# Moving two modulation vectors from the merges to the v, k and q projections

## The chip, the cores and the metric

The kernel runs on one core of a Trainium2 chip, in one launch. The metric is the device time of that launch in microseconds (us). TensorE (PE) does the matrix products and the transposes, VectorE (DVE) and ScalarE (ACT) the elementwise work, GpSimd (POOL) some sums and accumulating loads, and SyncE (SP) issues nearly all DMA transfers, in the order of its queue.

## The reference, cut to what matters

One layer of a diffusion backbone with 1024 latent tokens, 256 context tokens and width 1024, all in float32: a half-step feed-forward network, a mixer (short convolution beside attention of 8 query and 2 key heads, merged by gates), and a second half-step feed-forward network. Each part is normed and then shifted, scaled and gated by vectors made from a condition `c`.

```python
mod_lat = (jax.nn.silu(c) @ w_mod[layer] + b_mod[layer])[:, None, :]
ml = jnp.split(mod_lat, N_MOD, axis=-1)                     # nine vectors of 1024
...
hx = modulate(rms_norm(x, norm2_g[layer]), ml[3], ml[4])
bg_l, cg_l, vc_l, q_l, k_l, v_l, gt_l = jnp.split(hx @ w_in[layer], SPLITS, axis=-1)
...
o_l = latent_attention(q_l, k_all, v_all)
x = x + ml[5] * merge_branches(y_conv_l, o_l, gt_l, w_branch_conv[layer], w_branch_attn[layer], w_out[layer])
x = x + 0.5 * ml[8] * swiglu(modulate(rms_norm(x, norm3_g[layer]), ml[6], ml[7]),
                              ffn2_w_in[layer], ffn2_w_out[layer])
return rms_norm(x, final_g)
```

The change concerns `ml[6]` and `ml[7]`, the shift and the scale ahead of the second feed-forward network. They hang on `c` and `w_mod` alone, so they can be made at any time before that network's norm. Each is a row of 1024 times a matrix of 1024 x 1024.

## The kernel before, in words

**Number format.** Every product of matrices is made of three: operands are split into a high and a low part (`split`: ACT casts the high part, DVE subtracts it to get the low), and high x high, high x low and low x high are summed in PSUM (`mm3`).

**Stages.** First feed-forward network; its second product; the convolution's and the gates' projections (`mixed()`); the v, k and q projections; attention beside the convolution's output product; the merges of the two branches; the output projection with `w_out`; the second feed-forward network and the final norm.

**v.** Ten tiles of 128 tokens, 24 products of 128x256 each, into one of five PSUM banks of kind `s`; ACT and DVE split the result into `vc`, or `vh` and `vl`.

**k and q.** `heads()` yields eleven rounds of `heads2` (k of the context, k of two latent chunks, then q by four pairs of heads and two chunks). A round has three steps: the projections on PE, with a copy `xb` and squares on ACT; then the norm and rotary on DVE, with some products `hsw` on POOL; then PE's transposes of `xb`, pinned, and the read-out of the result. The steps of neighbouring rounds overlap by hand: the second step of a round is written ahead of the projections of the next one, and its third step behind them. Ahead of the last round, eight tiles `y` of the convolution are loaded.

**Attention's end.** For every 128 keys PE transposes four tiles of weights into one of two banks `pt`, ACT and DVE split them into `pts`, and PE multiplies them with v three times. At the end no scores are left to be made beside this, until the first merges (`ps<-oh`, `ps<-ol`) begin.

**Modulations.** `later_mod(m)` makes vector `m` in two halves of 512. For each half it goes over eight row blocks of `w_mod`: a block `rawm` of 128x512 is loaded (256 KB) and DVE adds it, times a column of `silu(c)`, to a sum `macc`. Then `macc` is split into `acch` and `accl`, two products with a column of ones sum it over the partitions (pinned), ACT copies the row out (`mrow`), a small DMA turns it into columns (`mcol`), and DVE adds the bias. It is a generator: eight steps of one block each, four empty ones, the split, six empty ones, the rest, 19 in all. So the code around it sets how thickly it is written between other work. `late_steps` runs it for vectors 6 and 7, 76 steps: four after each of 14 merges, then four after each of the first eight tiles of the output projection.

**Buffers.** Small tiles (`ttile`, 128x512) share 11 slots: `rawm`, `macc`, `acch`, `accl` and `mrow` here, and also `xb`, `hsw`, the merges' `ga` and `z`, attention's `qs` and `rrow`. Large tiles (`atile`, 128x1024) share 38 slots: the split inputs of the projections, v, k, q, `y`, the weights of attention. Weights have three slots `raw` of their own.

**Order.** A planner sets the order of the instructions on each engine and on SP when the program is built, from the dependencies, the slots and a timeline of its own. Work that isn't pinned may come ahead of the place where it is written. A pinned instruction stays behind all that was written before it for its engine. At run time each engine goes through its list in that order.

Of the kernel before, what the change touches and what calls it, by code (L numbers as in the profile page):

```python
# [18 lines left out]
P = 128  # L19
D = 1024  # L20
KD = D // P
# [14 lines left out]
C0, C1, CC = ("l", 0, 512), ("l", 512, 512), ("c", 0, CT)  # L36
# [15 lines left out]
def tile_dit_layer(  # L52
# [56 lines left out]
    def uniq(s):  # L109
        n_tiles[0] += 1  # L110
        return f"{s}_{n_tiles[0]}"

    def atile(name, shape=(P, SLOT), dt=F32):
        return apool.tile(list(shape), dt, tag="A", name=uniq(name))

    def ttile(name, n=512, dt=F32):
        t = tpool.tile([P, 512], dt, tag="t", name=uniq(name))
        return t[:, :n]

    def small(name, n, dt=F32):  # L120
        return spool.tile([P, n], dt, tag=f"s{n}_{name}", name=uniq(name))
# [4 lines left out]
    def ps_t(n=512):  # L126
        return psum.tile([P, 512], F32, tag="t", name=uniq("pt"), bufs=2)[:, :n]
# [4 lines left out]
    def matmul(out, w, x, start, stop, pinned=False, on=False):  # L132

        inst = pe.matmul(out, w, x, start=start, stop=stop, skip_group_check=on)
        if pinned:
            tc.keep_in_program_order(inst)
# [7 lines left out]
    def load(out, in_, pinned=False):  # L144
        inst = sp.dma_start(out=out, in_=in_)
        if pinned:
            tc.keep_in_program_order(inst)
# [38 lines left out]
    def col(name, k=0):  # L186
        o = voff[name] + k
        return cols[:, o : o + 1]
# [8 lines left out]
    def split(src, hi, lo, lo_eng=None, hi_eng=None):  # L197

        if hi_eng is dve:
            dve.tensor_copy(out=hi, in_=src)  # L200
        else:
            act.copy(out=hi, in_=src)
        (lo_eng or dve).tensor_sub(out=lo, in0=src, in1=hi.bitcast(F32))
# [65 lines left out]
            transpose(pr[:, j * P : (j + 1) * P], y[:, j : j + 1].to_broadcast([P, P]), pinned=True)  # L269
        return pr  # L270

    def later_mod(m, halves=(0, 1), streams=None):

        if streams is None:
            streams = (0, 1) if m < 5 else (0,)
        for half in halves:
            accs = [ttile(f"macc{v}") for v in streams]
            o = m * D + half * 512
            for k in range(KD):
                raw = ttile("rawm")  # L280
                load(out=raw, in_=w_mod[0, k * P : (k + 1) * P, o : o + 512])
                for acc, v in zip(accs, streams):
                    s = silu_c[:, v * 8 + k : v * 8 + k + 1]
                    if k == 0:
                        dve.tensor_scalar(out=acc, in0=raw, scalar1=s, scalar2=None, op0=ALU.mult)
                    else:
                        dve.scalar_tensor_tensor(out=acc, in0=raw, scalar=s, in1=acc, op0=ALU.mult, op1=ALU.add)
                yield
            for _ in range(WAIT):
                yield  # L290
            parts = []
            for acc in accs:
                ah, al = ttile("acch", dt=F32R), ttile("accl", dt=F32R)
                split(acc, ah, al)
                parts.append((ah, al))
            for _ in range(6):
                yield
            for (ah, al), v in zip(parts, streams):
                mod, pm = (modl, modc)[v], ps_t()
                matmul(pm[:1], ones_r[:], ah, start=True, stop=False, pinned=True)  # L300
                matmul(pm[:1], ones_r[:], al, start=False, stop=True, pinned=True)
                row = ttile("mrow")
                act.copy(
                    out=row[:1].rearrange("o (p j) -> o j p", j=4), in_=pm[:1].rearrange("o (j p) -> o j p", j=4)
                )
                mcol = small("mcol", 4)
                sp.dma_start(out=mcol[:], in_=row[:1])
                c0 = m * 8 + half * 4
                dve.tensor_add(out=mod[:, c0 : c0 + 4], in0=mcol[:], in1=bcol[:, c0 : c0 + 4])
            yield  # L310

    def fetch_mod(m, half):
        raws = []
        for kk in range(KD // 2):
            raw = atile("rawm", (P, 2, 512))
            o = m * D + half * 512
            load(raw[:], w_mod[0, kk * 256 : (kk + 1) * 256, o : o + 512].rearrange("(a p) n -> p a n", p=P), True)
            raws.append(raw)
        return raws

# [56 lines left out]
    def norm_gain(name, m, gname):  # L377

        g = {}
        for s in "l" if m >= 5 else "lc":  # L380
            g[s] = const.tile([P, 8], F32, name=f"{name}_{s}")
            part_gain(g[s], m, gname, s, 0, 8)
        return g

    def part_gain(t, m, gname, s, a, b):
        mod, c0, o = (modl if s == "l" else modc), (m + 1) * 8, voff[gname]
        dve.tensor_scalar(
            out=t[:, a:b], in0=mod[:, c0 + a : c0 + b], scalar1=1.0, scalar2=math.sqrt(D), op0=ALU.add, op1=ALU.mult
        )
        dve.tensor_mul(out=t[:, a:b], in0=t[:, a:b], in1=cols[:, o + a : o + b])  # L390
# [70 lines left out]
    def run(steps, n=None):  # L461

        if n is None:
            for _ in steps:
                pass
        else:
            for _ in range(n):
                next(steps, None)
# [597 lines left out]
    for k in range(4):  # L1066
        if k % 2:
            half1.shifted(h0[k][:, 0], k, xh[k])
        else:
            dve.tensor_scalar(  # L1070
                out=h0[k][:, 0], in0=xh[k], scalar1=gain1["l"][:, k : k + 1], scalar2=modl[:, k : k + 1],
# [53 lines left out]
    def all_later_mods():  # L1125
        yield from later_mod(1, (1,), (1,))
        yield from later_mod(0, (0, 1), (1,))
        part_gain(gain1["c"], 0, "g1", "c", 0, 8)
        for _ in normc:
            yield  # L1130
        for m in range(2, 5):
            yield from later_mod(m)

    steps = all_later_mods()
    mix_steps, late_steps, last_steps = later_mod(5), (step for m in (6, 7) for step in later_mod(m)), later_mod(8)


    hid_c = {}
# [91 lines left out]
    for d in range(0, KD, 2):  # L1230
# [8 lines left out]
        for e in range(2):  # L1239
            te = t[:, e * CT : (e + 1) * CT]  # L1240
            dve.scalar_tensor_tensor(
                out=te, in0=pt[:, e * CT : (e + 1) * CT], scalar=gate1["c"][:, d + e : d + e + 1], in1=te, op0=ALU.mult, op1=ALU.add
# [71 lines left out]
    for i in range(KD):  # L1314
# [6 lines left out]
        for ch, bg, gc in mixed():  # L1321
            gate(gcd, i, ch, gc)
            o = ch[1]
            y = ttile("y")
            dve.tensor_scalar(out=y, in0=u[:, o : o + 512], scalar1=col("w1", i), scalar2=None, op0=ALU.mult)
            for j in (0, 2):
                a, b = max(o, 1 - j), min(o + 512, L + 1 - j)
                ya = y[:, a - o : b - o]
                dve.scalar_tensor_tensor(
                    out=ya, in0=u[:, a + j - 1 : b + j - 1], scalar=col(f"w{j}", i), in1=ya, op0=ALU.mult, op1=ALU.add  # L1330
# [37 lines left out]
    def v_tile(kt):  # L1368
        if kt < 2:
            return v_ctx[:, kt], v_ctx[:, 2 + kt]  # L1370
        return v_hi[(kt - 2) // 4][:, (kt - 2) % 4], v_lo[(kt - 2) // 4][:, (kt - 2) % 4]

    for kt in range(10):
        ch = CC if kt < 2 else C0 if kt < 6 else C1
        o = (kt if kt < 2 else (kt - 2) % 4) * P
        pv_ = ps_s(256)
        proj_256(pv_, vw, ch, o)
        split(pv_, *v_tile(kt))


    rope_t = [atile("rope", (P, KD, HD)) for _ in range(2)]
# [94 lines left out]
    for i, h in enumerate(heads()):  # L1476
        run(before, 1)
        if i == NQ + 2:
            conv_weights(0)
            conv_weights(1)  # L1480
            conv_inputs(C0)
        run(h, 1)
        run(before)
        before = h
    run(before, 1)

    def conv_out(ch, j):

# [203 lines left out]
    for j in range(KD):  # L1692
        for ch in (C0, C1):
            if (j, ch) not in ((0, C0), (1, C0)):
                run(merge(j, ch))
                run(late_steps, 4)
    xs = Latents("x2")
    fast = Winograd(xs, None, modl, 6, column_pairs(ffn2_w_in[0], ffn_offsets), ahead=AH3)
    first = fast.norm0()
    for ch in (C0, C1):  # L1700
        o = ch[1]
        for d in range(KD):
            w = load_cols(w_out[0], d * P)
            load(xs(d, ch), xd[d, :, o : o + 512])
            ps = ps_s()
            mm3(ps, [
                (w[0][:, k], w[1][:, k], m_hi[k][:, o : o + 512], m_lo[k][:, o : o + 512]) for k in range(KD)
            ])
            dve.scalar_tensor_tensor(
                out=xs(d, ch), in0=ps, scalar=modl[:, 40 + d : 41 + d], in1=xs(d, ch), op0=ALU.mult, op1=ALU.add  # L1710
            )
            if ch == C0:
                run(late_steps, 4)
                if d == KD - 1:
                    fast.gain = norm_gain("gain3", 6, "g3")["l"]
            if ch == C1:
                fast.square(d)
                if d in (0, 1):
                    run(first, 1)
                if d == 2:  # L1720
                    run(first)
# [5 lines left out]
        out=gf[:], in0=cols[:, voff["gf"] : voff["gf"] + 8], scalar1=math.sqrt(D), scalar2=None, op0=ALU.mult  # L1727
# [132 lines left out]
```

## Time and profile before

| what | value |
|---|---|
| median of three runs | 2684.68 us (2680.94, 2684.68, 2685.43) |
| profiled execution | 2685.79 us, of it the span 2684.0 us |
| mean granted clock of TensorE | 0.995 |
| v tiles | about 1290 to 1320 us |
| k and q rounds | about 1320 to 1465 us |
| attention | about 1460 to 1859 us |
| merges | about 1836 to 1931 us |
| output projection | about 1931 to 2021 us |
| `macc` for vectors 6 and 7, first and last start | 1813.3 and 1951.6 us |

All times of the profile are counted from the first instruction of the span. In a timeline row stand the start, the time the row covers, the engine, the operation, out<-in by the program's names, the shapes and the count; in square brackets the time for which the engine was idle before it and what ended that idle time. A PE row's length is that of a pipelined product, so products follow each other more closely than their lengths say: the distance of two starts is what one costs. SPq and POOLq are the queues that issue DMA transfers. Every instruction carries line 90, since a helper records it, so rows are told apart by the names of their tiles.

### The profile page before, as it was taken

The numbers are of one execution on the slowest core, as the hardware profiler recorded it, in microseconds if no ns is written. First come the engines' busy times: TensorE is split into PE (matmuls) and PEld (weight loads), VectorE is DVE, ScalarE is ACT, GpSimd is POOL, SyncE is SP. The second block draws the span as 40 slices with busy tenths as digits, with TensorE's granted clock in tenths as the row PEclk, the third lists the DMA queues.
The fourth block names the chain that finished last, engine by engine and source line by source line (L and its number), as shares of the span: only waits on it lengthen the run. The fifth ranks groups of instructions, "written<-read, shape, count | busy, mean of one in ns | idle before, by whom it ended". The sixth has DMA issues, their size and how long they took to land.

```text
span 2684.0 us, 36956 instructions
## 1 busy us (share of the span) xinstructions
PE 2639.7 (98%) x13373; PEld 2221.6 (83%) x13373; DVE 2006.2 (75%) x3356; ACT 1171.3 (44%) x2317; POOL 557.9 (21%) x449
## 2 busy tenths in 40 slices
PE   8999999999999999999999999999999999999998
PEld 5787899888778878888999888887888788888888
DVE  5788966888877899877387676675668876667885
ACT  6533454433444633333245566673236233334453
POOL 0134201211010044333032112141001442330200
PEclk9999999999999999999999999999999999999999
DMA  8565465345974345242312532113734543228741
GB/s 317 194 204 177 144 221 173 109 130 209 288 182 122 111 158 180 95 130 75 103 48 91 87 87 64 32 44 110 262 100 144 181 154 95 86 88 288 182 90 64
DMA packets 370000, 376.93 MB, mean 140 GB/s; under 512 B 19590, under 2 KB 258328, under 8 KB 369816
## 3 DMA queue, kind: packets, MB, share of 16 engines
q1 hardware_dynamic: 359000, 353.03, 40.8%
q0 software_dynamic: 10816, 21.53, 4.9%
q8 instruction: 105, 1.72, 0.3%
q14 instruction: 79, 0.65, 0.1%
HBM read 306.78 MB, written 67.67 MB: 140 GB/s over the span
## 4 chain that ended last, share of the span: by engine, by line
PE 84%; DVE 4%; DMA 2%; issue 2%; POOL 1%; ACT 1%; SPq 0%; DVEq 0%; POOLq 0%; ACTq 0%
PE ps L90 69%; PE pt L90 7%; PE po L90 7%; DVE wl L90 1%; DMA raw<-in_ffn_w_in_dram 1%; DMA ws<-in_ffn_w_out_dram 1%; DVE r L90 1%; DMA rawm<-in_w_mod_dram 1%; POOL s L90 0%; DVE macc L90 0%; POOL ol L90 0%; DVE u L90 0%; DVE uc L90 0%; DVE nt L90 0%; DVE v L90 0%
## 5 line engine op out<-in xcount | busy, mean ns | idle before, releaser
L90 PE MATMUL ps<-r,wl 128*128 128x512 f32 x5196 | 1204.7, 391 | 12.2 <-DVE wl L90 5.3
L90 PEld LDWEIGHTS ps<-r,wl 128*128 128x128 f32 x5196 | 971.6, 188 | 221.9 <-DVE wl L90 7.9
L90 ACT CAST wl<-s 128x512 fp32r<-128x512 f32 x254 | 156.7, 619 | 322.6 <-PE ps L90 219.3
L90 POOL TENSOR_TENSOR s<-raw 128x512 f32<-128x512 f32 x64 | 93.4, 1459 | 891.2 <-DMA raw<-in_ffn_w_in_dram 380.9
L90 ACT CAST wl<-raw 128x512 fp32r<-128x512 f32 x287 | 177.5, 619 | 219.6 <-PE ps L90 157.3
L90 DVE TENSOR_TENSOR wl<-raw,wl 128x512 fp32r<-128x512 f32 x287 | 201.9, 705 | 62.1 <-ACT wl L90 59.6
L90 DVE TENSOR_TENSOR wl<-s,wl 128x512 fp32r<-128x512 f32 x254 | 229.8, 905 | 21.3 <-ACT wl L90 19.7
L90 POOL TENSOR_TENSOR s<-raw,s 128x512 f32<-128x512 f32 x64 | 103.9, 1624 | 362.3 <-DVE wl L90 362.3
L90 DVE SCALAR_TENSOR_TENSOR macc<-rawm,silu_c,macc 128x512 f32<-128x512 f32 x178 | 149.8, 858 | 31.7 <-DMA rawm<-in_w_mod_dram 30.7
L90 PE MATMUL ps<-wh,r 128*128 128x256 f32 x768 | 141.6, 285 | 0.0
L90 DVE TENSOR_TENSOR u<-u,ps 128x512 f32<-128x512 f32 x174 | 118.0, 678 | 28.7 <-PE ps L90 28.5
L90 DVE TENSOR_TENSOR pts<-pt,pts 128x512 fp32r<-128x512 f32 x160 | 108.7, 685 | 35.7 <-ACT pts L90 33.5
L90 ACT CAST pts<-pt 128x512 fp32r<-128x512 f32 x160 | 93.3, 595 | 94.8 <-PE pt L90 90.9
L90 DVE TENSOR_REDUCE m<-ps 128x1 f32<-128x512 f32 (+1 forms) x192 | 109.9, 594 | 23.3 <-PE ps L90 22.3
L90 ACT CAST rh<-hid 128x512 fp32r<-128x512 f32 x132 | 80.9, 620 | 101.6 <-PE ps L90 89.3
L90 PE MATMUL ps<-rh,wl 128*128 128x512 f32 x360 | 122.3, 390 | 2.8 <-ACT rh L90 2.8
L90 PEld LDWEIGHTS ps<-wh,r 128*128 128x128 f32 x768 | 120.6, 192 | 0.0
L90 PE MATMUL po<-pts,vh 128*128 128x512 f32 x256 | 111.4, 440 | 0.2 <-ACT pts L90 0.2
L90 PE MATMUL ps<-wl,r 128*128 128x256 f32 x384 | 108.8, 283 | 0.0
L90 ACT CAST wh<-raw 128x512 fp32r<-128x512 f32 (+1 forms) x85 | 67.9, 801 | 88.8 <-PE ps L90 57.8
L90 DVE TENSOR_TENSOR rl<-hid,rh 128x512 fp32r<-128x512 f32 x132 | 89.8, 684 | 20.2 <-PE ps L90 9.8
L90 PE MATMUL ps<-kl,qs 128*128 128x512 f32 x384 | 104.3, 395 | 0.0
(314 smaller groups left out, 5118.6 us busy)
## 6 DMA issues: line engine op xcount, KB each, us to landing
raw<-in_ffn_w_in_dram SPq DMA_DIRECT2D x130, 512.0 KB
raw<-in_ffn_w_out_dram SPq DMA_DIRECT2D x72, 512.0 KB
rawm<-in_w_mod_dram SPq DMA_DIRECT2D x136, 256.0 KB
raw<-in_w_in_dram SPq DMA_DIRECT2D x61, 512.0 KB
hid<-hd SPq DMA_DIRECT2D x40, 512.0 KB
ws<-in_ffn_w_out_dram POOLq DMA_DIRECT2D x30, 512.0 KB, 6.6
ucd<-uc SPq DMA_DIRECT2D x25, 512.0 KB
hd<-c SPq DMA_DIRECT2D x40, 256.0 KB
```

What stands on the lines that cost most here:

```text
L90: inst = getattr(self.engine, name)(*args, **kw)
```

## The change

The generator gets a second way to load: with `by_four` a half fetches its eight row blocks at once, by four loads of 512 KB into four large tiles, and its steps then only compute. Vectors 6 and 7 take this way, and their steps move: three after each of the ten v tiles, five after each of the eleven rounds of k and q, and what is left behind them. They are taken out of the merges and of the output projection, and the gain made from vector 7 is formed ahead of the output projection. `fetch_mod`, until now used for the first vectors with pinned loads, gets a switch for unpinned ones.

```diff
-    def later_mod(m, halves=(0, 1), streams=None):
+    def later_mod(m, halves=(0, 1), streams=None, by_four=False):
...
         for half in halves:
+            raws = fetch_mod(m, half, False) if by_four else None
             accs = [ttile(f"macc{v}") for v in streams]
             o = m * D + half * 512
             for k in range(KD):
-                raw = ttile("rawm")
-                load(out=raw, in_=w_mod[0, k * P : (k + 1) * P, o : o + 512])
+                if by_four:
+                    raw = raws[k // 2][:, k % 2]
+                else:
+                    raw = ttile("rawm")
+                    load(out=raw, in_=w_mod[0, k * P : (k + 1) * P, o : o + 512])
...
-    def fetch_mod(m, half):
+    def fetch_mod(m, half, pinned=True):
         raws = []
         for kk in range(KD // 2):
             raw = atile("rawm", (P, 2, 512))
             o = m * D + half * 512
-            load(raw[:], w_mod[0, kk * 256 : (kk + 1) * 256, o : o + 512].rearrange("(a p) n -> p a n", p=P), True)
+            load(raw[:], w_mod[0, kk * 256 : (kk + 1) * 256, o : o + 512].rearrange("(a p) n -> p a n", p=P), pinned)
             raws.append(raw)
         return raws
...
-    mix_steps, late_steps, last_steps = later_mod(5), (step for m in (6, 7) for step in later_mod(m)), later_mod(8)
+    mix_steps, late_steps, last_steps = later_mod(5), (step for m in (6, 7) for step in later_mod(m, by_four=True)), later_mod(8)
...
         proj_256(pv_, vw, ch, o)
         split(pv_, *v_tile(kt))
+        run(late_steps, 3)
...
         run(h, 1)
         run(before)
+        run(late_steps, 5)
         before = h
     run(before, 1)
+    run(late_steps)
...
                 run(merge(j, ch))
-                run(late_steps, 4)
     xs = Latents("x2")
     fast = Winograd(xs, None, modl, 6, column_pairs(ffn2_w_in[0], ffn_offsets), ahead=AH3)
     first = fast.norm0()
+    fast.gain = norm_gain("gain3", 6, "g3")["l"]
...
-            if ch == C0:
-                run(late_steps, 4)
-                if d == KD - 1:
-                    fast.gain = norm_gain("gain3", 6, "g3")["l"]
```

## The prediction

> **What bounds the kernel now.** I read the page first, then the busy time by stretches, the timeline of TensorE (PE) around each place where it was not busy, and what VectorE (DVE) and the load queue (SP) did there.
>
> ```profile
> PE 2639.7 (98%) x13373; PEld 2221.6 (83%) x13373; DVE 2006.2 (75%) x3356; ACT 1171.3 (44%) x2317; POOL 557.9 (21%) x449
> ...
> 1290.00:1326.00 36.00, 36.00 (x300) 35.90 (x299) 9.25 (x17) 7.03 (x15) 0.00 (x0) 1.00 0.34 111
> 1326.00:1466.00 140.00, 140.00 (x1113) 136.91 (x1113) 111.33 (x297) 64.49 (x231) 42.00 (x80) 1.00 0.19 60
> 1798.00:1820.00 22.00, 19.18 (x110) 14.83 (x108) 12.58 (x25) 13.05 (x29) 13.67 (x10) 1.00 0.30 71
> 1820.00:1842.00 22.00, 19.67 (x93) 15.54 (x94) 13.94 (x20) 8.21 (x14) 1.60 (x2) 0.84 0.30 86
> 1850.00:1934.00 84.00, 84.00 (x372) 69.07 (x371) 55.62 (x80) 24.13 (x32) 1.46 (x1) 1.00 0.63 205
> 1934.00:2022.00 88.00, 88.00 (x395) 72.46 (x395) 53.57 (x84) 35.35 (x50) 0.00 (x0) 1.00 0.44 139
> 2081.00:2091.50 10.50, 7.56 (x30) 5.07 (x29) 9.61 (x13) 4.22 (x8) 3.26 (x3) 1.00 0.20 76
> ```
>
> A row gives the stretch and its length, the busy time of PE, weight loads, DVE, ACT and POOL, then the granted clock and the DMA share. The stretches are v (to 1326), k and q (to 1466), the end of attention (1798 to 1842), the merges (to 1934) and the output projection (to 2022). PE is full in all but the end of attention: only time taken from PE counts, and the new place and most of the old one have none to give back. In 1798 to 1842 it is idle 2.82 + 2.33 = 5.15 us, and the clock column falls to 0.84. That is where the moved work now begins, before the merges after which it is written:
>
> ```profile
> 1806.94 0.60 PE L90 MATMUL pt<-ident,pl 128*128 128x128 f32 x4
> 1811.48 0.60 PE L90 MATMUL pt<-ident,pc 128*128 128x128 f32 x4
> 1817.47 0.40 PE L90 MATMUL po<-pts,vh 128*128 128x512 f32 x1
> 1821.51 1.11 PE L90 MATMUL pt<-ident,pl 128*128 128x128 f32 x4 [3.64 <-DVE pts L90]
> 1823.70 1.06 PE L90 MATMUL pt<-ident,pl 128*128 128x128 f32 x4
> 1825.83 1.05 PE L90 MATMUL pt<-ident,pl 128*128 128x128 f32 x4
> 1827.80 0.60 PE L90 MATMUL pt<-ident,pl 128*128 128x128 f32 x4
> 1836.61 0.39 PE L90 MATMUL ps<-ol,wh 128*128 128x512 f32 x1
> 1837.59 0.66 PE L90 MATMUL pt<-ident,pl 128*128 128x128 f32 x4 [0.59 <-DVE pts L90]
> 1845.91 0.40 PE L90 MATMUL po<-pts,vh 128*128 128x512 f32 x1
> 1846.43 0.63 PE L90 MATMUL pt<-ident,pl 128*128 128x128 f32 x4
> ...
> 1815.55 0.69 DVE L90 TENSOR_TENSOR pts<-pt,pts 128x512 fp32r<-128x512 f32 x1 [1.13 <-ACT pts L90]
> 1819.43 1.42 DVE L90 SCALAR_TENSOR_TENSOR macc<-rawm,silu_c,macc 128x512 f32<-128x512 f32 x1 [3.19 <-DMA rawm<-in_w_mod_dram]
> 1820.78 0.68 DVE L90 TENSOR_TENSOR pts<-pt,pts 128x512 fp32r<-128x512 f32 x1
> 1836.19 0.75 DVE L90 SCALAR_TENSOR_TENSOR macc<-rawm,silu_c,macc 128x512 f32<-128x512 f32 x1 [1.07 <-DMA rawm<-in_w_mod_dram]
> ...
> 1815.48 1.30 POOL L90 TENSOR_TENSOR q<-q,rrow 128x512 f32<-128x512 f32 x1
> 1816.81 0.33 SPq L90 DMA_DIRECT2D rawm<-in_w_mod_dram  x1
> ...
> PE pt L90 <- DVE pts L90: 4.5, 3, 3.6
> DVE macc L90 <- DMA rawm<-in_w_mod_dram: 10.3, 6, 3.3
> ```
>
> Read it backwards. PE stands 3.64 us before the transposes at 1821.51, because their PSUM bank is read out by pts on DVE at 1820.78. That pts stands behind a macc, which waited 3.19 us for its row. The row's load left SP at 1816.81, as soon as the POOL product of 1815.48 had ended at 1816.78 and freed a small buffer. So a load without a buffer holds DVE, and DVE holds PE. Afterwards the rounds of transposes come 2.1 us apart until 1827.80, where they had come 1.135 us apart (1806.94 to 1811.48 is four rounds); the clock is down.
>
> **What the old place gives back.** First wait: 1821.51 less 1817.47 is 4.04, less the 0.24 that one product takes, 3.80. Slow rounds: 1821.51 to 1827.80 is 6.29 for three rounds, less 3 x 1.135 = 3.41, so 2.88. Second wait, behind the macc of 1836.19: 0.98 less 0.24, 0.74. Third, 1845.91 to 1846.43: 0.52 less 0.24, 0.28. Sum 7.70 us. The upper bound is all idle time there plus the slow rounds, 5.15 + 2.88 + 0.28 = 8.31; the lower is nothing, if pts meets another holder at once. I take 7.70, since each of these waits has a macc directly ahead of pts and the rounds before 1812 run evenly without one. What is late next is the 1.135 us round itself, and from 1850 on PE is full, so time gained here reaches the end.
>
> The other three of the four halves (each 8 rows) run beside full PE and give nothing: their waits for rows are covered by the merges' and output projection's products, and that cover is left behind, not taken along.
>
> **What the new place is charged.**
>
> ```profile
> L90 DVE SCALAR_TENSOR_TENSOR macc<-rawm,silu_c,macc x28: 734/751/1419, 1819.4 to 1951.6; 128x512 f32<-128x512 f32 x28
> L90 DVE TENSOR_SCALAR macc<-rawm,silu_c x4: 477/479/486, 1813.3 to 1942.9; 128x512 f32<-128x512 f32 x4
> L90 DVE TENSOR_TENSOR accl<-macc,acch x4: 677/688/694, 1863.5 to 1953.0; 128x512 fp32r<-128x512 f32 x4
> L90 PE MATMUL pt<-acch,ones_r x4: 397/397/397, 1881.4 to 1959.0; 128*1 128x512 f32 x4
> L90 ACT COPY mrow<-pt x4: 1069/1073/1079, 1882.0 to 1960.0; 1x512 f32<-1x512 f32 x4
> ...
> 1409.47 0.69 DVE L90 TENSOR_TENSOR xb<-xb,hsw 128x512 f32<-128x512 f32 x1
> 1412.86 0.17 DVE L90 TENSOR_SCALAR ssa<-ss 128x8 f32<-128x8 f32 x1 [2.69 <-ACT hsq L90]
> 1410.63 0.38 PE L90 MATMUL pt<-ident,xb 128*128 128x128 f32 x2
> 1412.29 0.82 PE L90 MATMUL pt<-ident,xb 128*128 128x128 f32 x6
> ...
> 1424.83 1.52 SPq L90 DMA_DIRECT2D y<-yd  x3
> 1433.08 2.22 SPq L90 DMA_DIRECT2D y<-yd  x5
> ...
> L90 ACT CAST vh<-ps x8: 373/373/373, 1299.3 to 1319.5; 128x256 fp32r<-128x256 f32 x8
> ```
>
> DVE gets 28 x 0.751 + 4 x 0.479 + 4 x 0.688 = 25.7 us. It is idle 26.8 us of the 36 of the v stretch and 28.7 of the 140 after it. Three steps follow each of ten v tiles, 30 of the 76; a half is 19 steps, so the first 16 rows fall to v, where five PSUM banks stand between PE and DVE and nothing else of weight waits. The other 16 rows come five steps per round of k and q. A round has a DVE chain that must end before PE turns its result: here at 1410.16, 2.13 us before the six transposes at 1412.29, and then DVE waits 2.69 us for the next round's squares. Five rows are 3.75 us, so even written out as they stand they exceed that idle time by 1.1, inside 2.13. Cost 0 there, and 3.75 per round if the cover is gone.
>
> A late row is the real price. The nearest rows are DVE's waits above, 3.19 and less, made by loads that got their buffer late. One such wait inside a round costs PE 3.19 less 2.13 = 1.1 us; none costs 0 (no gain is possible beside a PE full 140 of 140 us). Buffers: the y loads show how many large ones are left late in q. Three go at once from 1424.83, the other five only from 1433.08; so about three of 38 are free there, and more earlier, before q's tiles take theirs. A half needs four. I take one wait, 1.1 us, for a half that has to queue; the upper end stands under the rivals.
>
> The remaining edits. SP: 32 issues of 0.33 us and more become 16, put ahead of weight loads, the rope tables and, at the end, y; SP mostly waits for slots there, so 0. PE: the eight one-column products move without a change of count. ACT: four row copies of 1.07 and four splits move to where ACT is busy 64.5 of 140, 0; a copy ahead of the squares would delay the chain by 1.07, inside 2.13. The row's way back (a 2 KB load and an add on DVE) moves with it. gain3 is formed before the output projection instead of in it: two DVE operations, 0. The small buffers freed in the merges serve loads that PE does not wait for now: 0.
>
> **Sum.** The profiled execution took 2685.79 us (span 2684.0 and 1.79 around it): 2685.79 - 7.70 + 1.1 = 2679.19. It stands 1.11 over the median of the runs shown, 2684.68, so the median to come is 2678.1; I write 2678. The change by 6.6 us is little over 0.2% (5.4 us), about what a measurement of this kernel can tell from no change.
>
> **The rivals.**
>
> *The slow rounds are not there in the middle run.* Without them the old place gives 4.82, less 1.1: 2684.68 - 3.7 = 2681, the same within 0.2%. For it: the three runs spread over 4.5 us (2680.94 to 2685.43), as if one had gone without them. Against it: the profiled run has them and is near the median. [...]
>
> *The gain is given back by a wait elsewhere.* The planner orders everything after 1290 anew. The 10.5 us from 2081 hold 2.94 us of idle PE with DVE busy 9.61: one more such place, or pts held by something else in the end of attention, and the time is 2681 to 2685, the same. It could as well vanish, which sets the low end.
>
> *Slower: PE waits at the sums of a half.* The two one-column products of each half are pinned behind the tile or round before them, six steps after the split of the sums. In the old place 5.3 us or more lie between (the last accl starts at 1953.0 and takes 0.69, its product starts at 1959.0). In v six steps are two tiles of 2.89 us (vh, 1299.3 to 1319.5 in seven), 5.8 us, so little more. If the rows of a half land late, PE stands there as at 1821.51, and nothing passes. One event costs 3.80 + 2.88 = 6.7. One undoes the gain; two of the four halves decide it: 2684.68 - 7.7 + 13.4 = 2690. For it: four loads of 512 KB arrive together, and DVE's order has put rows ahead of other work that landed 3 us later. Against it: the loads ask for large buffers, of which many are free when v begins, and a 0.34 DMA share leaves room.
>
> That the change does not take the loads out of the end of attention cannot be: their steps are used up (30 + 55 is more than 76).
>
> **How the numbers follow.** Forecast 0.50, no slow rounds to win 0.14, given back elsewhere 0.20, slower 0.16. Faster 0.50, same 0.34, slower 0.16. Low end: 2678 less the 2.94 of 2081 less the 1.1 charged, 2674, and 1 for the runs' scatter, 2673. High end: into the slower case, one event and a half, 2687, and 1 for scatter, 2688; the forecast alone is 2675 to 2681.
>
> **What would show it.** Right: no rawm load after 1466 but those of the last gate; pts rounds of 1.135 us through 1810 to 1836 with the clock at 1.00; PE still full to 1466; merges beginning some 7 us earlier. Wrong: PE idle before xb transposes or before the acch products; y loads or weights late on SP; a wider gap near 2081; or rounds that stay slow with pts behind something else.

## The result, and the profile after

The median went from 2684.42 us (nine runs, 2680.61 to 2687.02) to 2676.78 us (nine runs, 2674.01 to 2681.00), ratio 0.9971 [0.9962, 0.9981]: 7.6 us less. The forecast was 2678. Runs of one kernel differ by some 7 us; after, the fastest, 2674.01 us, has a granted clock of 0.997, the slowest, 2681.00 us, one of 0.994. The profiled execution took 2677.21 us, its span 2675.3 against 2684.0.

The page's row of busy time and the busy time by stretches, of the kernel after (columns as before):

```profile
PE 2637.8 (99%) x13373; PEld 2222.0 (83%) x13373; DVE 2007.0 (75%) x3356; ACT 1172.3 (44%) x2317; POOL 557.1 (21%) x449
...
1290.00:1326.00 36.00, 36.00 (x294) 35.48 (x293) 21.56 (x36) 9.33 (x17) 0.00 (x0) 1.00 0.66 223
1326.00:1466.00 140.00, 140.00 (x1116) 136.72 (x1115) 119.25 (x316) 68.77 (x235) 41.78 (x80) 1.00 0.27 89
1798.00:1820.00 22.00, 21.31 (x125) 16.95 (x124) 13.60 (x26) 15.15 (x37) 12.40 (x11) 1.00 0.22 55
1820.00:1842.00 22.00, 21.76 (x124) 17.77 (x123) 12.44 (x19) 10.64 (x18) 3.64 (x2) 1.00 0.18 55
1850.00:1934.00 84.00, 84.00 (x372) 69.58 (x371) 43.12 (x57) 20.75 (x27) 1.46 (x1) 1.00 0.53 169
2022.00:2100.00 78.00, 75.08 (x336) 61.01 (x336) 66.75 (x106) 37.70 (x65) 18.39 (x12) 1.00 0.49 158
```

No engine has less to do: the counts of instructions are the same and PE's busy time fell by only 1.9 us. In the end of attention PE is idle 0.69 + 0.24 = 0.93 us where it was idle 5.15, and the clock column stands at 1.00 where it stood at 0.84. DVE's work has moved: 21.56 against 9.25 us in v, 119.25 against 111.33 in k and q, 43.12 against 55.62 in the merges. PE is full in v, k and q as before.

The end of attention after, from the timeline of PE, with the wait of PE for `pts` from the chain of waits of 1798 to 1862:

```profile
1817.00 0.60 PE L90 MATMUL pt<-ident,pl 128*128 128x128 f32 x4
...
1826.09 0.60 PE L90 MATMUL pt<-ident,pc 128*128 128x128 f32 x4
...
PE pt L90 <- DVE pts L90: 0.2, 1, 0.2
```

Eight rounds lie between the two rows, 9.09 us or 1.136 each: the even pace, over the very stretch in which the kernel before stood still for 3.64 us and then ran at half pace, 2.10 us a round. The wait of PE for `pts` is down from 4.5 us in three to 0.2 in one.

A measure that can be read from every run is the end of attention itself: the distance from the last product with `kl` (scores) to the last product with `vh`. The groups of the two tiles, first for the kernel before, then after (the last number before the semicolon is the start of the group's last instruction):

```profile
L90 PE MATMUL ps<-kl,qs x384: 387/393/499, 1459.9 to 1799.3; 128*128 128x512 f32 x192
L90 PE MATMUL po<-pts,vh x256: 389/402/775, 1496.2 to 1858.5; 128*128 128x512 f32 x128
```

```profile
L90 PE MATMUL ps<-kl,qs x384: 387/393/486, 1462.8 to 1802.0; 128*128 128x512 f32 x192
L90 PE MATMUL po<-pts,vh x256: 388/401/502, 1499.1 to 1852.9; 128*128 128x512 f32 x128
```

Before it is 1858.5 - 1799.3 = 59.2 us, after it is 1852.9 - 1802.0 = 50.9: 8.3 less in one profile of each, with the slowest `po` product at 502 ns where it was 775. The last score itself comes 2.7 us later and what follows the last `vh` product is 3.1 us shorter (2684.0 - 1858.5 = 825.5 and 2675.3 - 1852.9 = 822.4). Most of that pair is the eight one-column products, 0.23 us each (two of them take 1311.75 to 1312.21 after), 1.8 together, now done before attention; the rest is within the scatter of the runs.

One more measure leaves most of the scatter out. The first 6267 and the last 3341 products come in the same order on PE in both kernels, so what differs lies between the 6267th product (`ps<-wh,r`, 1310.5 us before) and the 3341st from the end (`ps<-ml,wh`, 1961.1 us before). That stretch takes 650.6 us in this profile of the kernel before, 649.3 in a second one shown below, and 642.4 after: 8.2 or 6.9 less.

### The profile page after: what moved, and what is told of

Its sections match the earlier page's. It is cut to its first block, busy times and chain, and to the rows that moved or that the text cites. A ratio compares the mean times of both kernels' runs of the same rounds, so it can differ in the third digit from the quotient of the medians.

```text
span 2675.3 us, 36939 instructions
## 1 busy us (share of the span) xinstructions
PE 2637.8 (99%) x13373; PEld 2222.0 (83%) x13373; DVE 2007.0 (75%) x3356; ACT 1172.3 (44%) x2317; POOL 557.1 (21%) x449
## 4 chain that ended last, share of the span: by engine, by line
PE 92%; DVE 4%; issue 1%; DMA 1%; ACT 1%; POOL 0%; SPq 0%; DVEq 0%; POOLq 0%; ACTq 0%
PE ps L90 76%; PE po L90 8%; PE pt L90 8%; DVE r L90 1%; DVE wl L90 1%; DVE nt L90 0%; DVE macc L90 0%; DMA rawm<-in_w_mod_dram 0%; DVE uc L90 0%; POOL s L90 0%; DMA raw<-in_ffn_w_in_dram 0%; DMA ws<-in_ffn_w_out_dram 0%; DVE v L90 0%; DVE y L90 0%; DMA mcol<-mrow 0%
```

## The experiments

My theory: nothing but the first half of vector 6 in attention's end matters, and what it costs there is a late row that holds DVE, hence `pts`, hence PE, hence the clock. The rivals: the large buffers and 512 KB loads bring the gain; taking three halves out of the merges and the output projection brings it; it is DVE's work itself, not the wait; and, for the new place, that the spread in v and the rounds is what keeps it free. Below, "attention's end" is the distance measured above.

**Nothing moved, one instruction pinned.** The kernel before, with the first sum of vector 6's first half kept behind what is written before it on DVE, so that the half can't start early:

```diff
                     if k == 0:
+                        strict[0] = m == 6 and half == 0
                         dve.tensor_scalar(out=acc, in0=raw, scalar1=s, scalar2=None, op0=ALU.mult)
+                        strict[0] = False
```

> The kernel before, with one instruction held: the first sum of vector 6's first half is pinned on DVE behind what is written before it, so that its eight sums cannot come into attention's end. Loads, buffers and place stay. Theory (a sum that waits for its row holds pts, pts holds PE, the clock falls): no macc before about 1860, PE idle in 1798 to 1842 falls from 5.15 us to about 1, clock there 1.00, time 7 us lower, 2677. Rival 1 (the gain is the work taken out of the merges and the output projection, or the moved loads): nothing is taken out, so 2684. Rival 2 (the large buffers bring it): 2684.

2678.16 us against 2683.94, ratio 0.9980 [0.9971, 0.9988]. The groups of the first sums and of the two tiles, this kernel:

```profile
L90 DVE TENSOR_SCALAR macc<-rawm,silu_c x4: 479/482/486, 1868.2 to 1941.2; 128x512 f32<-128x512 f32 x4
...
L90 PE MATMUL ps<-kl,qs x384: 387/393/486, 1464.2 to 1803.5; 128*128 128x512 f32 x192
L90 PE MATMUL po<-pts,vh x256: 387/401/497, 1500.6 to 1854.3; 128*128 128x512 f32 x128
```

The first sum starts at 1868.2 instead of 1813.3, and attention's end takes 50.8 us, as with the change. The loads keep their size, their buffers and their place in the program, though with the sums seven of the eight loads also leave SP later, from 1858.67. By the medians 5.8 of the 7.6 us are there, and the two intervals overlap. The stretch between the 6267th and the 3341st last product takes 642.5 us here, against 642.4 with the change. So the gain comes from when the first half starts.

**Three halves moved, the first left behind.** The kernel after, but vector 6's first half with its small loads stays in the merges:

```diff
-    mix_steps, late_steps, last_steps = later_mod(5), (step for m in (6, 7) for step in later_mod(m, by_four=True)), later_mod(8)
+    mix_steps, late_steps, last_steps = later_mod(5), (step for m in (7, 6) for step in later_mod(m, (0, 1) if m == 7 else (1,), by_four=True)), later_mod(8)
+    first_half = later_mod(6, (0,))
...
                 run(merge(j, ch))
+                run(first_half, 4)
```

> The changed kernel, with vector 6's first half alone left in the merges with its eight small loads; the other three halves are made beside v, k and q. Theory: the first half comes into attention's end as before, with its wait and its slow rounds, so the time stays that of before, 2684 (2682 to 2686). Rival 1 (the gain is work taken out of the merges and the output projection): three quarters of it, 2679.

2682.93 us, ratio 0.9998 [0.9989, 1.0007]: no change from the kernel before, with three quarters of the move done. The groups of the two tiles and PE's transposes:

```profile
L90 PE MATMUL ps<-kl,qs x384: 386/393/487, 1462.0 to 1801.2; 128*128 128x512 f32 x192
L90 PE MATMUL po<-pts,vh x256: 388/402/776, 1498.4 to 1857.4; 128*128 128x512 f32 x128
...
1822.60 1.12 PE L90 MATMUL pt<-ident,pl 128*128 128x128 f32 x4 [2.91 <-DVE pts L90]
1824.80 0.96 PE L90 MATMUL pt<-ident,pl 128*128 128x128 f32 x4
1826.29 0.60 PE L90 MATMUL pt<-ident,pl 128*128 128x128 f32 x4
```

PE stands 2.91 us for `pts` and then runs a round of 2.20 and one of 1.49 us. Attention's end is 56.2 us: the stop and the slow rounds are there, 1.8 to 3.0 us cheaper than in the two profiles of the kernel before. The other three halves give nothing that the medians show, as the prediction had it; the interval allows some 3 us.

**Large loads at the old place.** The kernel before, with `by_four` in `late_steps` and nothing moved:

```diff
-    mix_steps, late_steps, last_steps = later_mod(5), (step for m in (6, 7) for step in later_mod(m)), later_mod(8)
+    mix_steps, late_steps, last_steps = later_mod(5), (step for m in (6, 7) for step in later_mod(m, by_four=True)), later_mod(8)
```

> The kernel before with the new way of loading at the old place: four loads of 512 KB into large slots per half. Theory: what counts is whether a sum with a late row stands ahead of pts in attention's end. If the large slots are taken by attention's weights until its end, the first half starts after it and the time is 2677; if they let the loads in early, the rows are there and the waits are short, 2677 to 2681. A macc wait over 3 us ahead of pts would give 2684. Rival 1 (work taken out of the merges): 2684 with no wait to be seen.

2677.79 us, ratio 0.9976 [0.9966, 0.9986]. SP's first load, the first sums and the two tiles:

```profile
1851.16 2.10 SPq L90 DMA_DIRECT2D rawm<-in_w_mod_dram  x4
...
L90 DVE TENSOR_SCALAR macc<-rawm,silu_c x4: 475/479/486, 1858.8 to 1933.4; 128x512 f32<-128x512 f32 x4
...
L90 PE MATMUL ps<-kl,qs x384: 387/393/486, 1463.7 to 1803.0; 128*128 128x512 f32 x192
L90 PE MATMUL po<-pts,vh x256: 388/401/499, 1500.0 to 1853.8; 128*128 128x512 f32 x128
```

The first half's loads stand behind the weight loads in SP's queue here and leave at 1851.16, its sums start at 1858.8, and attention's end is 50.8 us. I had expected attention's hold on the large slots to delay them; the trace shows no wait for a slot, so why the planner put them there is open. Taken alone this looks as if large buffers brought the gain. The pinned kernel above and the next one say otherwise: they help only because the half starts late with them.

**Small loads at the new place.** The kernel after, without `by_four`, so 32 loads of 256 KB into the small slots:

```diff
-    mix_steps, late_steps, last_steps = later_mod(5), (step for m in (6, 7) for step in later_mod(m, by_four=True)), later_mod(8)
+    mix_steps, late_steps, last_steps = later_mod(5), (step for m in (6, 7) for step in later_mod(m)), later_mod(8)
```

> The changed kernel with the old way of loading: 32 loads of 256 KB into the 11 small slots, steps at the new place. Theory (place decides, buffers do not): attention's end is free, 2677, plus up to 1.1 us for each DVE wait over 2.1 us inside a round of k and q, since rows again wait for small slots: 2677 to 2681. Rival 2 (the large buffers bring it): rows come late into the rounds, PE waits at xb or at the sums, 2684 or more.

2675.36 us (five runs), ratio 0.9965 [0.9953, 0.9978], as fast as the change. The waits of DVE for rows in v, k and q, and the two tiles:

```profile
DVE macc L90 <- DMA rawm<-in_w_mod_dram: 5.4, 7, 1.9
...
L90 PE MATMUL ps<-kl,qs x384: 386/393/487, 1461.0 to 1800.2; 128*128 128x512 f32 x192
L90 PE MATMUL po<-pts,vh x256: 388/402/497, 1497.3 to 1851.0; 128*128 128x512 f32 x128
```

DVE waits seven times for a row, 5.4 us in all, and the time does not show it: PE is busy for all of the 176 us from 1290 to 1466, so in this stretch these late rows cost nothing. The place matters, not the size of the loads.

**The sums at the old place, with no row to wait for.** The kernel before; vector 6's first half is summed from data already on the chip, and the eight rows of `w_mod` for it are left out:

```diff
-                raw = ttile("rawm")
-                load(out=raw, in_=w_mod[0, k * P : (k + 1) * P, o : o + 512])
+                if m == 6 and half == 0:
+                    raw = units[-1].pl[0][:, :512]
+                else:
+                    raw = ttile("rawm")
+                    load(out=raw, in_=w_mod[0, k * P : (k + 1) * P, o : o + 512])
```

> The kernel before, with vector 6's first half summed from a tile of attention's weights that is in SBUF already, in place of eight rows of w_mod that are loaded (so that half of the vector isn't what it should be). The eight sums, 5.7 us of DVE, may still come into attention's end; no row is waited for. Theory (the wait for the row, not the sum's own 0.75 us, holds pts): PE stands for no more than one sum at a time, under 0.75 us, the clock stays 1.00, time 2677 to 2679. Rival (DVE's added work in attention's end is what PE waits for): the time stays near 2684.

2679.27 us against 2683.85, ratio 0.9988 [0.9979, 0.9997]: a gain, but about 2.5 us short of the change, and PE stopped for longer than I expected. The timelines of DVE, POOL and PE:

```profile
1816.16 0.74 DVE L90 SCALAR_TENSOR_TENSOR macc<-pl,silu_c,macc 128x512 f32<-128x512 f32 x1
1817.42 1.76 DVE L90 SCALAR_TENSOR_TENSOR macc<-pl,silu_c,macc 128x512 f32<-128x512 f32 x1
1820.55 0.68 DVE L90 TENSOR_TENSOR pts<-pt,pts 128x512 fp32r<-128x512 f32 x1
1821.15 2.27 DVE L90 SCALAR_TENSOR_TENSOR macc<-pl,silu_c,macc 128x512 f32<-128x512 f32 x1
...
1817.33 1.29 POOL L90 TENSOR_TENSOR q<-q,rrow 128x512 f32<-128x512 f32 x1
1820.16 2.71 POOL L90 TENSOR_TENSOR ol<-q,oh 128x1024 fp32r<-128x1024 f32 x1
...
1819.84 0.66 PE L90 MATMUL pt<-ident,pl 128*128 128x128 f32 x4 [0.57 <-DVE pts L90]
1824.07 0.66 PE L90 MATMUL pt<-ident,pl 128*128 128x128 f32 x4 [1.43 <-DVE pts L90]
...
L90 PE MATMUL ps<-kl,qs x384: 387/393/486, 1462.6 to 1801.9; 128*128 128x512 f32 x192
L90 PE MATMUL po<-pts,vh x256: 388/401/495, 1498.9 to 1855.6; 128*128 128x512 f32 x128
```

A sum takes 0.74 us here, but 1.76 and 2.27 us where it lies beside a POOL operation on two tiles. The `pts` behind it is late by that much, and PE waits 0.57 and 1.43 us. No slow round follows: the clock of 1820 to 1842 is 1.00, and the round from 1824.07 takes 1.26 us. Attention's end is 53.7 us. So the 8.3 us of the two profiles split: 59.2 - 53.7 = 5.5 hang on the late rows, with the slow rounds that followed their stop of 3.64 us, and 53.7 - 50.9 = 2.8 on the sums themselves. With the 58.0 us of the second profile of before the first part is 4.3. The medians give 4.6 and 2.5; the interval alone would not tell this kernel from the pinned one, so the split rests on the profiles. No run has the loads early and the sums late, so that the loads alone cost nothing is not tested.

**The steps only in the rounds.** The kernel after without the steps behind the v tiles, and seven instead of five per round:

```diff
         split(pv_, *v_tile(kt))
-        run(late_steps, 3)
...
-        run(late_steps, 5)
+        run(late_steps, 7)
```

> The changed kernel with no steps behind the v tiles and seven in place of five behind each round of k and q. Theory (a round has 2.7 us of idle DVE and 2.1 us of slack before PE turns its result): where eight sums fall into little more than one round, 5.3 us against 4.8, PE waits about 0.5 us in some four rounds, and a late row costs more: 2677 to 2681, with the idle PE to be seen before xb. Rival (the order finds room in other rounds, and slack does not bind): 2677 and PE full to 1466.

2681.25 us (eleven runs, 2675.26 to 2685.93), ratio 0.9990 [0.9981, 0.9998]: some 4 us of the gain are lost, but not where I looked. PE does not wait before the transposes of `xb`. It waits once, after the last round. PE, then ACT, in the profiled run:

```profile
1459.77 0.50 PE L90 MATMUL ps<-kc,qs 128*128 128x256 f32 x2 [1.83 <-ACT qs L90]
...
1457.28 1.05 ACT L90 CAST wc<-raw 128x1024 fp32r<-128x1024 f32 x1 [1.45 <-PE ps L90]
1458.23 1.06 ACT L90 COPY mrow<-pt 1x512 f32<-1x512 f32 x1
1459.09 0.63 ACT L90 CAST qs<-q 128x512 fp32r<-128x512 f32 x1
```

The last half now ends with the last round. Its row copy `mrow` (1.06 us) and a cast stand on ACT ahead of the cast `qs` that attention's first scores need. That profiled run was the fastest of the eleven. Two more profiles of the same kernel and one more of the kernel before follow.

> The kernel before once more, for its profile. Theory: PE stands between 3 and 4 us before a transpose near 1818 behind a macc that waits for its row, and slow rounds follow, for 2 to 3 us of loss. Rival (the slow rounds are rare): the wait without them, clock 1.00 in 1820 to 1842, and a time near 2681.

> The dense kernel once more, for a second profile: its eleven times run from 2675 to 2686 and the profile at hand is of the fastest. Theory (a late row in a round of k and q holds the chain behind it): DVE waits for rawm by more than 2.1 us inside a round and PE stands before xb or before the sums, 3 to 8 us in 1326 to 1480 in all. Rival (the order is sound and the scatter lies in the first 1000 us): PE idle no more than 2.2 us in 1326 to 1466, as in the first profile.

> As the run before it, a third profile: theory, the loss in 1326 to 1480 grows with the time of the run; rival, it stays at some 3 us and the first 1000 us differ.

They took 2686.27 (before), 2679.78 and 2681.47 us; the kernel before, run beside the last two, took 2686.65. The theory of a late row inside a round fails and the rival holds: from 1326 to 1466 PE is idle for 1.83 and 1.84 us in the second and third profile, 2.17 in the first, and the loss does not grow with the time of the run. The stop of 1.83 us is in all three profiles of the dense kernel. In the second it is followed by slow products (PE):

```profile
1461.70 0.60 PE L90 MATMUL ps<-kc,qs 128*128 128x256 f32 x2 [1.83 <-ACT qs L90]
1462.10 1.91 PE L90 MATMUL ps<-kl,qs 128*128 128x512 f32 x4
1463.81 0.42 PE L90 MATMUL ps<-kc,qs 128*128 128x256 f32 x1
1464.02 1.06 PE L90 MATMUL ps<-kl,qs 128*128 128x512 f32 x2
1464.88 1.31 PE L90 MATMUL ps<-y,wc 128*128 128x512 f32 x4
```

The four products of the second row take 1463.81 - 1462.10 = 1.71 us, 0.43 each, where one costs 0.24 with the clock at 1.00 (`po<-pts,vl` to the next product before, 1806.48 to 1806.72), and one of half the width 0.12 (24 of them in the 2.89 us of a v tile). From 1461.70 to 1464.88 these six products and three of half the width take 3.18 us instead of 7.5 x 0.24 = 1.80, so some 1.4 us are lost; the other two profiles have nothing of the kind. So the stop and the slow products cost 1.8 to 3.2 us.

Again the order of PE's products bounds the loss. It is the same as with the change up to the 6267th product (1311.6 us after) and in the last 5814 (from 1478.3 after). Between the two lie 166.7 us after, and 169.7, 170.3 and 169.5 in the three dense profiles: 2.8 to 3.6 more, which is mostly the stop, the slow products and small waits of the next scores for `qs` (0.25 us in the first profile). What is left of the 4.5 us between the medians 2681.25 and 2676.78 lies where PE's order is the same. There the dense profiles differ among themselves as well: the 6267th product starts at 1306.8, 1308.8 and 1311.7, so 4.9 of the 6.2 us between their spans arise ahead of the point where the order differs.

The second profile of the kernel before shows the same stop with the same holder, and slow rounds that begin later (PE):

```profile
1823.59 0.66 PE L90 MATMUL pt<-ident,pl 128*128 128x128 f32 x4 [3.08 <-DVE pts L90]
1825.15 1.05 PE L90 MATMUL pt<-ident,pl 128*128 128x128 f32 x4
1827.29 0.82 PE L90 MATMUL pt<-ident,pl 128*128 128x128 f32 x4
1828.66 0.60 PE L90 MATMUL pt<-ident,pl 128*128 128x128 f32 x4
```

Its three rounds are 1.56, 2.14 and 1.37 us, a loss of 5.07 - 3.41 = 1.66 where the first profile lost 2.88.

## Why the prediction was right, point by point

**What the old place gives back: right, 7.70 forecast.** Attention's end is 8.3 us shorter than in the first profile of the kernel before. In the second its rows give 58.0, so 7.1 by that. The stretch with another order of products gives 8.2 and 6.9. All the signs asked for are there: even rounds, the clock at 1.00, PE's wait all but gone. That the sum of four terms fits this closely is in part luck: the two profiles of before differ by 1.3 us in this stretch.

**Its cause: right in the main, one part mis-sized.** I put the whole 7.70 down to late rows. The sums alone, without any wait, cost 2.8 us of attention's end. The sign stood in a row I had quoted: the `macc` of 1819.43 took 1.42 us where the group's median is 0.751, and I counted its 0.67 us of excess as part of the wait. It ran beside this POOL operation of the kernel before:

```profile
1817.97 2.34 POOL L90 TENSOR_TENSOR ol<-q,oh 128x1024 fp32r<-128x1024 f32 x1
```

A repair that only loaded the rows earlier, at the old place, would have fallen short by that much.

**The slow rounds: there each time, of changing size.** 2.88 and 1.66 us in the two profiles of before, about 1.4 with three halves moved. The rival that the middle run goes without them is not borne out, though not excluded either: both profiles of before are of runs above its median (2685.79 and 2686.27 against 2683.9). Against the rival speaks that the profile with three halves moved shows them, with 2680.6 us against that kernel's median of 2682.93.

**The other three halves: right, within some 3 us.** Moving them gave 0.9998 [0.9989, 1.0007].

**The new place: forecast 1.1, found 0.** This is the term that was off. DVE's only wait for a row, the loads on SP's queue, the sums of the first half and their product, and the round that takes the fourth half, all after:

```profile
1301.27 0.49 DVE L90 TENSOR_SCALAR macc<-rawm,silu_c 128x512 f32<-128x512 f32 x1 [2.89 <-DMA rawm<-in_w_mod_dram]
1308.75 0.69 DVE L90 TENSOR_TENSOR accl<-macc,acch 128x512 fp32r<-128x512 f32 x1 [1.02 <-ACT acch L90]
...
1294.08 5.03 SPq L90 DMA_DIRECT2D rawm<-in_w_mod_dram  x6
...
1378.98 4.09 SPq L90 DMA_DIRECT2D rawm<-in_w_mod_dram  x4
...
1311.75 0.40 PE L90 MATMUL pt<-acch,ones_r 128*1 128x512 f32 x1
...
1400.51 0.68 DVE L90 TENSOR_TENSOR xb<-xb,hsw 128x512 f32<-128x512 f32 x1
1403.09 0.82 PE L90 MATMUL pt<-ident,xb 128*128 128x128 f32 x6
```

The late row came, 2.89 us of it, close to the 3.19 I had bounded it by. But it came in v, on the first row of all, where the PSUM banks stand between DVE and PE and PE is busy for 36.00 of 36.00 us, and not inside a round. The last half was fetched at 1379, ahead of the `y` loads that I had taken as the measure of free buffers. Two loads of the second half did come late, for a reason that the prediction had not looked at: they left SP at 1314.08, some 15 us behind the rest, because the small DMA `mcol` of the first half stood before them in SP's queue and waited for its `mrow` (1312.4 to 1313.5; `mcol` left at 1313.52). DVE did not wait for them. From 1395 to 1406 DVE takes a whole half, eight sums, four of them ahead of the end of the round's chain. That chain still ends 1403.09 - 1401.19 = 1.90 us before the transposes; in the same round before it is 1399.06 - 1397.08 = 1.98 (the 2.13 of the prediction is of the round behind it).

**The slower rival: not met, and not by much.** The first half's `accl` ended at 1309.44 and its first product started at 1311.75, a margin of 2.3 us behind a row that came 2.89 us late. The experiment with everything in the rounds shows the price of this kind of edge: there a row copy stood ahead of the first scores and PE stopped for 1.83 us.

**Given back elsewhere: no.** The 78 us from 2022, with the gap near 2081 in them, have PE busy for 75.08 us after (75.06 before), and the merges stay full. The forecast came out 1.2 us high, about the charge of 1.1; but the interval of the ratio, 5.1 to 10.2 us less, is far too wide for the medians to show that.

## What to carry to other kernels

When a stage of full engines has one stretch with a stop, go back from the stop through the in-order queues to the first late thing. The place to mend may be a single instruction: here one pinned sum gave what a move of 76 steps gave: all of it by the profiles, 5.8 of 7.6 us by the medians. Work that waits for a DMA and may come early can land in a tight chain of an in-order queue; put it where a bank or buffer stands between that queue and the engine that counts, as in v, where a row 2.89 us late left PE full. Price such work there by what its operations take beside the other engines in that very stretch, not by their median: the sum with a median of 0.751 us took 1.42 in the end of attention.

## What the runs showed of the hardware that I had not expected

**Sums on DVE stretched beside POOL, the read-out `pts` did not.** With nothing loaded for them, `macc<-pl,silu_c,macc`, with two inputs in SBUF, went from 0.74 to 1.76 and 2.27 us beside POOL's operations on two tiles; `pts<-pt,pts`, with one input in PSUM, started at 1820.55 inside POOL's 2.71 us from 1820.16 and kept its 0.68. In the kernel before the `macc` of 1819.43 took 1.42 us beside POOL's 2.34 us from 1817.97, and the `pts` of 1815.55 took 0.69 beside POOL's 1.30 us from 1815.48. What makes the difference the rows do not show.

**The clock fell behind some stops and not behind others of the same length.** Stops of 3.64, 3.08 and 2.91 us in attention's end were all followed by slow products (the clock of 1820 to 1842 is 0.84, 0.92 and 0.92). A stop of 1.83 us was followed by nine of them, to 3.2 us after it, in one of three profiles and by none in the other two (the clock of 1326 to 1466 is 0.99, and 1.00 in both others), and one of 1.43 us (with 0.57 us shortly before it) by none (1.00). Stops far ahead of the change, where PE's order is the same before and after, go both ways as well:

| stop of PE, near | before, and the clock behind it | after, and the clock behind it |
|---|---|---|
| 30 us | 1.32 us, then 0.48; 0.76 (30.2 to 34) | 1.32 us, then 0.48; 0.81 (30.2 to 34) |
| 92 us | 2.34 us, 1.00 (91.8 to 95) | 2.31 us, 0.65 (93.1 to 96) |
| 744 us | 2.84 us, 1.00 (743.2 to 747) | 2.84 us, 0.51 (746 to 749.4) |
| 955 us | 2.79 us, 1.00 (954.7 to 957) | 2.79 us, 1.00 (955.7 to 958) |

Near 2080 a stop of 1.60 us before and 1.61 after left the clock at 1.00. So in these profiles the length of a stop alone does not tell whether the clock falls. That is part of why runs differ: behind the stop near 744 the same twelve products take 746.29 - 743.20 = 3.09 us before and 749.44 - 744.80 = 4.64 after. The 1.1 us charged to the new place counted no slow products behind such a wait of PE; no run had one there, so that it leaves the clock alone was not shown, and the stops near 30, of 1.32 us and half a microsecond, with a clock below 1.00 behind them in both profiles, speak against taking it for granted.
